# Pooling products in three rounded parts, and the new tokens' small transposes padded to 128 rows

## The chip, the cores and the metric

The kernel runs on one core of a Trainium2 chip. The metric is the device time of one execution in microseconds (us); the time given for a kernel is the median of its runs.

## What is computed

One inference step of a decoder with a single layer, for a prompt of 1024 positions and for 8 new tokens (one for each of 8 samples). The input is normalised and projected; the columns of the projection go to an attention group (three branches: compressed blocks, selected blocks, window) and to a pooling group; each is gated, both are projected back, added to the input and normalised. The change touches the pooling group, the attention of the new tokens, and the positional rows of the compressed branch. Cut from the reference:

```python
def pool_mixer(u_ext, n_out, w_pool, pool_scale):
    ...
    mean = (csum[:, le - n_out + 1:] - lo) / (end[:, None] - start).astype(f32)
    d = (mean - uf[:, le - n_out:]).reshape(n, n_out, N_POOL_GROUPS, POOL_GROUP_DIM)
    y = jnp.einsum('nlgc,gcd->nlgd', d, w_pool).reshape(n, n_out, D_POOL)
    return y * pool_scale

def block(bi):                                   # of nsa_attention
    ...
    p_c = jnp.where(ok_c, jax.nn.softmax(jnp.where(ok_c, s_c, -MASK_BIG), axis=-1), 0.0)
    o_c = jnp.einsum('nkgqc,nckd->nqkgd', p_c, v_c)
    ...
    o_s = jnp.einsum('nkgqs,nkqsd->nqkgd', p_s, vg)
    ...
    o_w = jnp.einsum('nkgqs,nskd->nqkgd', p_w, wrows[:, :, 1])
    return gg[..., 0:1] * o_c + gg[..., 1:2] * o_s + gg[..., 2:3] * o_w
```

For the pooling group there are four groups of 128 channels with windows of 2, 4, 8 and 16 positions and one 128 x 128 matrix each. A new token attends to 256 cached positions in each of the selected and the window branch and to itself.

## The kernel before

Data lie with features or tokens on the 128 partitions. Products of full precision are made from rounded parts: a float32 value is copied to a rounded type (the high part, on ScalarE) and the rest is subtracted (the low part, on VectorE or GpSimd; `split_w`, lines 138 to 140), and a product is the sum of high by high, low by high and high by low, three TensorE instructions. A few products stay in plain float32: the pooling products and some small ones of the new tokens. The trace shows a plain float32 product as two passes.

The stages in order of time: the input is normalised and transposed, and keys, values and gates are projected token by token (0 to 109 us); keys and values are compressed (to 194 us); the queries are projected (lines 490 to 505); then, from about 194 to 293 us, the four pooling groups, with the attention of the new tokens in between; then the attention over the prompt in 32 units (8 tiles of 128 queries by 4 pairs of heads), with the gate path (lines 918 to 948) and the output projection as filling work, to the end.

A pooling group (loop from line 761) loads a tile of projection weights, projects 1032 tokens (1024 and the 8 new ones) in three chunks of 384, 384 and 264 columns (`feat_unit`, lines 359 to 367), adds up windows on VectorE, takes the differences `dd` (line 792), projects its gate in three chunks, and multiplies `dd` with its matrix `pw`, chunk by chunk (line 809). The result is scaled, gated and stored.

The attention of the new tokens (`decode`, lines 509 to 662) runs at a raised priority ahead of the pooling in the program. It makes scores of the compressed branch (line 570), a softmax, and a transpose of it (575); then for each of the other two branches it transposes the new keys (586), gathers the cached rows of 8 samples, two at a time, in buffers `kvx` (599 to 605), transposes the keys (607), splits keys and values (612 to 618), makes the scores (621, 622), a softmax, transposes it (632) and its column for the new token (634), and multiplies with the values (645) and the new value (653). The sum is transposed at the end (656). The transposes at 575, 632, 634 and 656 have 64 rows (8 samples by 8 heads), the one at 586 has 8, and that of the positional rows (409) has 32.

The order on each engine is made by a planner that simulates a time line from costs of its own and takes what is ready by priority; instructions then run in that order on each engine, each waiting for its inputs. So a change of some costs can move the order of other work too. Loads from memory go through SP's queue in order, gathers through GpSimd's. A tile that reuses the memory of an earlier one waits for that one's last readers. The first attention unit's softmax tiles lie where the new tokens' tiles lay.

Of the kernel before, what the change touches and what calls it, by code (L numbers as in the profile page):

```python
# [22 lines left out]
# pacing of the filling products: steps per block of attention (gate path, output), blocks added per unit,  # L23
# steps at the start, lag in products
# [3 lines left out]
# the rows of the output weights, by half of their columns, that take the place of each chunk of x  # L28
# [13 lines left out]
def hybrid_step_kernel(ctx, tc, xp, xs, ccmp, cslc, cwin, spool, ptab, norm_g, w_in, cmp_pe, cmp_w1,  # L42
# [34 lines left out]
    # DRAM scratch  # L77
# [5 lines left out]
    # constants  # L83
# [8 lines left out]
    def ptr_rms(pool, ssq, n, name):  # L92
        """(ssq / D + eps) ** -0.5 for a [n, 1] column."""
# [5 lines left out]
    # persistent data  # L99
# [56 lines left out]
    pe32 = keep.tile([32, 128], F32, name="pe32")  # L156
# [7 lines left out]
    nc.sync.dma_start(pe32, cmp_pe)  # L164
    def spread_g(h):
        """The norm's weights from the first partition to all."""
        cs = slice(h * 512, h * 512 + 512)
        p = ps_any()
        nc.tensor.matmul(p, ones, gb[0:1, cs], start=True, stop=True)
        if h:  # L170
            nc.scalar.activation(gb[:, cs], p, AF.Copy)
        else:
            nc.vector.tensor_copy(gb[:, cs], p)

    # masks
# [12 lines left out]
    # normalised x, transposed, as high and low parts  # L188
# [37 lines left out]
    # token-major projections: compressed, selected and window keys and values, gate logits  # L226
# [114 lines left out]
    # a token before the end of the first compressed block has no compressed branch  # L341
# [28 lines left out]
    def silu2(out, src):  # L370
        """2 * silu(src)"""
# [3 lines left out]
    # page indices: row of 2 tokens each  # L375
# [12 lines left out]
    # compressed keys and values, prompt and samples  # L388
# [20 lines left out]
    nc.tensor.transpose(p[:, :32], pe32, ident[:32, :32])  # L409
# [79 lines left out]
    # queries  # L489
# [19 lines left out]
    def decode():  # L509
        """One new token per sample."""  # L510
        dp = des.enter_context(tc.tile_pool(name="dp", bufs=1, reuse_waits="tile"))
        # queries, one column per head and sample; qx: high parts, then low parts, per sample
# [7 lines left out]
        def diag(ap):  # L520
            """The columns of each sample's own heads in [b, 2, 64] columns: [p, b, h]."""
# [15 lines left out]
        for br in range(2):  # L537
            kn = dp.tile([NB, 256], F32, name=f"knew{br}")
            nc.sync.dma_start(kn, (nslc_s, nwin_s[:, 255])[br])
# [18 lines left out]
        Pd = [dp.tile([64, 258], F32, name=f"pd{br}") for br in range(2)]  # L558
        Pd = [Pd[0], Pd[1], Pd[0]]
# [15 lines left out]
        nc.tensor.transpose(p[:, :64], Pd[0][:, :128], ident[:64, :64])  # L575
        PcT = dp.tile([128, 64], F32, name="PcT")
        nc.vector.tensor_copy(PcT, p[:, :64])
        od = dp.tile([64, 128], F32, name="od")
# [3 lines left out]
        for br in range(2):  # L582
            vx = []
            kn = dp.tile([128, NB], F32, name="kn", bufs=2)
            p = ps_s("dkn")
            nc.tensor.transpose(p[:, :NB], knew[br][:, :128], ident[:NB, :NB])
            nc.vector.tensor_copy(kn, p[:, :NB])
            sp = ps_s("dS")
            for b in range(0, NB, 2):
# [8 lines left out]
                for bb in range(2):  # L598
                    f = dp.tile([128, 512], F32, name="kvx", bufs=4)
# [9 lines left out]
                    # high and low parts of the values  # L609
# [18 lines left out]
            dd = dp.tile([64, NB], F32, name="dd", bufs=2)  # L628
            nc.vector.tensor_scalar(dd, bmask, P_[:, 256:257], None, op0=OP.mult)
            p = ps_s("dptr")  # L630
            for par in range(2):
                nc.tensor.transpose(p[:, par * 64:(par + 1) * 64], P_[:, par * 128:(par + 1) * 128],
                                    ident[:64, :64])
            nc.tensor.transpose(p[:NB, 128:192], dd, ident[:64, :64])
            for par in range(2):
                src = p[:, par * 64:(par + 1) * 64].rearrange("p (b h) -> p b h", b=NB)
# [3 lines left out]
            E_ = dp.tile([NB, 64], F32, name="dE", bufs=2)  # L640
            nc.vector.tensor_copy(E_, p[:NB, 128:192])
# [11 lines left out]
            nc.tensor.matmul(p[:64, :128], E_, knew[br][:, 128:256], start=True, stop=True)  # L653
            nc.vector.tensor_add(od, od, p[:64, :128])
        p = ps_s("dOt")
        nc.tensor.transpose(p[:, :64], od, ident[:64, :64])
# [548 lines left out]
```

## Time and profile before

| | us |
|---|---|
| median of 3 runs | 656.16 |
| lowest, highest | 655.71, 656.98 |
| the profiled execution: span from the first to the last instruction | 654.4 |
| TensorE products busy | 627.6 (96%) |
| TensorE weight loads busy | 581.6 (89%) |
| VectorE busy | 426.0 (65%) |
| ScalarE busy | 361.0 (55%) |
| GpSimd busy | 266.8 (41%) |

The profile is of one execution; its own time is not given beside its span, so the median stands for it, 1.8 us above the span. Busy time counts the modelled length of an instruction, and products overlap in it. In the rows, PE is TensorE, DVE is VectorE, ACT is ScalarE, POOL is GpSimd, SP is the engine whose queue issues most loads; L809 is line 809; `out<-in` names the tiles written and read; of a product, `64*128` gives the rows and columns of its weights and `64x64` the rows and columns that are streamed.

### The profile page before, as it was taken

How to read it: one execution, taken by the hardware profiler on the slowest of the kernel's cores; microseconds unless marked ns; L12 is line 12 of the kernel's file. 1: busy time of each engine (PE TensorE's matmuls, PEld its weight loads, DVE VectorE, ACT ScalarE, POOL GpSimd, SP SyncE). 2: the span in 40 equal slices, each digit the busy share in tenths (PEclk: the TensorE clock that was granted, in tenths of full speed). 3: DMA queues.
4: the chain of work that ended last, by engine and by line, in shares of the span. 5: the costliest groups of instructions: out<-in, count | busy, mean ns of one | idle time of the engine just before them, and what ended most of it. 6: DMA issues, size and time to landing. Idle time of an engine off the chain costs nothing. (4 is left out here: it accounts for less than half of the span.)

```text
span 654.4 us, 12214 instructions
## 1 busy us (share of the span) xinstructions
PE 627.6 (96%) x4141; PEld 581.6 (89%) x4141; DVE 426.0 (65%) x1306; ACT 361.0 (55%) x930; POOL 266.8 (41%) x410
## 2 busy tenths in 40 slices
PE   6995999999999999999999899999999999999995
PEld 4995999999999999998999888788899999988984
DVE  5741234555526547575797998779888788877652
ACT  5652233444413234325788787767587677665641
POOL 5153001431207424104565666736454445454511
PEclk9997999999999999999999999999999999999999
DMA  8432302984524342243313437212022030101001
GB/s 274 147 100 56 102 16 76 310 274 118 162 72 135 84 142 70 94 132 98 97 33 98 130 113 238 86 34 82 32 83 97 18 97 18 65 17 66 18 34 64
DMA packets 65677, 65.14 MB, mean 100 GB/s; under 512 B 6423, under 2 KB 56927, under 8 KB 65575
## 3 DMA queue, kind: packets, MB, share of 16 engines
q1 hardware_dynamic: 55599, 44.53, 22.8%
q0 software_dynamic: 3968, 12.76, 6.0%
q10 hardware_dynamic: 6048, 7.08, 3.0%
q8 instruction: 33, 0.54, 0.3%
q14 instruction: 29, 0.24, 0.1%
HBM read 50.99 MB, written 15.68 MB: 102 GB/s over the span
## 5 line engine op out<-in xcount | busy, mean ns | idle before, releaser
L756 POOL TENSOR_SCALAR Ps<-Ps,sm,gates 128x64 f32<-128x64 f32 (+1 forms) x120 | 75.3, 639 | 111.1 <-DVE sm L752 77.3
L736 PE MATMUL S<-KT,qt 128*128 128x320 f32 (+10 forms) x400 | 98.3, 347 | 1.9 <-DVE sm L699 1.8
L859 DVE TENSOR_TENSOR pl<-tp,ph 128x512 fp32r<-128x512 f32 (+1 forms) x136 | 89.9, 670 | 13.5 <-ACT ph L858 12.4
L858 ACT ACTIVATE ph<-tp 128x512 fp32r<-128x512 f32 (+1 forms) x136 | 76.6, 579 | 35.2 <-PE tp L853 28.2
L365 PE MATMUL pa<-x,ws_hi 128*128 128x384 f32 (+1 forms) x288 | 93.6, 325 | 0.0
L366 PE MATMUL pa<-x,ws_hi 128*128 128x384 f32 (+1 forms) x288 | 92.8, 322 | 0.0
L367 PE MATMUL pa<-x,ws_lo 128*128 128x384 f32 (+1 forms) x288 | 92.6, 322 | 0.0
L750 ACT ACTIVATE Ps<-Ps,sm 128x64 f32<-128x64 f32 (+8 forms) x128 | 70.6, 554 | 28.2 <-DVE sm L748 26.7
L995 PE MATMUL pj<-wo,mh 128*128 128x512 f32 x256 | 82.6, 400 | 0.0
L871 PE MATMUL O<-pl,V 128*128 128x256 f32 x264 | 77.7, 311 | 1.0 <-DVE pl L859 0.9
L870 PE MATMUL O<-ph,V 128*128 128x256 f32 x264 | 74.2, 295 | 0.0
L736 PEld LDWEIGHTS S<-KT,qt 128*128 128x128 f32 x400 | 63.9, 189 | 8.8 <-DVE sm L699 2.8
L244 PE MATMUL pa<-w_hi,x 128*128 128x256 f32 (+1 forms) x192 | 57.7, 301 | 0.2 <-DVE V L317 0.2
L246 PE MATMUL pa<-w_hi,x 128*128 128x256 f32 (+1 forms) x192 | 56.9, 296 | 0.4 <-DVE x L217 0.4
L245 PE MATMUL pa<-w_lo,x 128*128 128x256 f32 (+1 forms) x192 | 56.1, 293 | 0.0
L366 PEld LDWEIGHTS pa<-x,ws_hi 128*128 128x128 f32 x288 | 54.2, 188 | 0.4 <-issue 0.2
L365 PEld LDWEIGHTS pa<-x,ws_hi 128*128 128x128 f32 x288 | 54.2, 188 | 0.3 <-DVE us L776 0.2
L367 PEld LDWEIGHTS pa<-x,ws_lo 128*128 128x128 f32 x288 | 54.1, 188 | 0.3
L871 PEld LDWEIGHTS O<-pl,V 128*128 128x128 f32 x264 | 49.7, 188 | 4.8 <-DVE pl L859 3.0
L870 PEld LDWEIGHTS O<-ph,V 128*128 128x128 f32 x264 | 49.9, 189 | 2.0 <-ACT ph L858 0.2
L995 PEld LDWEIGHTS pj<-wo,mh 128*128 128x128 f32 x256 | 45.1, 188 | 7.0 <-PE S L736 0.4
L995 PE MATMUL pj<-wo,ml 128*128 128x512 f32 x128 | 50.6, 395 | 0.1
(279 smaller groups left out, 1530.9 us busy)
## 6 DMA issues: line engine op xcount, KB each, us to landing
ws_raw<-in_w_in SPq DMA_DIRECT2D x32, 256.0 KB
qt<-q_d SPq DMA_DIRECT2D x64, 128.0 KB
x_t<-in_x_prompt SPq DMA_DIRECT2D x8, 512.0 KB
wo_raw<-in_w_out SPq DMA_DIRECT2D x8, 512.0 KB
r<-in_x_prompt SPq DMA_DIRECT2D x8, 512.0 KB
out<-r SPq DMA_DIRECT2D x7, 512.0 KB
q_d<-qhl ACTq DMA_DIRECT2D x8, 384.0 KB
out<-kvf ACTq DMA_DIRECT2D x5, 512.0 KB
```

The source lines that it names most:

```text
L244: nc.tensor.matmul(p[:n, :cn], xh[c][:, k, ts_], hi[:, k, :cn], start=k == 0, stop=False)
L365: nc.tensor.matmul(p[:, :n], hi[:, k, :], xh[c][:, k, :], start=k == 0, stop=False)
L366: nc.tensor.matmul(p[:, :n], hi[:, k, :], xl[c][:, k, :], start=False, stop=False)
L367: nc.tensor.matmul(p[:, :n], lo[:, k, :], xh[c][:, k, :], start=False, stop=k == 7)
L736: nc.tensor.matmul(S[:, :ln], qt[:, f, h, :], KT[:, kv, k0 + a:k0 + a + ln], start=f == 0, stop=f == 1)
L750: nc.scalar.activation(regs[br], regs[br], AF.Exp, bias=sm[:, hh, 1, br:br + 1], accum_out=sm[:, hh, 2, br:br + 1])
L756: nc.gpsimd.tensor_scalar(regs[br], regs[br], sm[:, hh, 3, br:br + 1], gsrc[:, k:k + 1], op0=OP.mult, op1=OP.mult)
L858: nc.scalar.activation(ph[:, :m], tp[:, :m], AF.Copy)
L859: nc.vector.tensor_sub(pl[:, :m], tp[:, :m], r32(ph[:, :m]))
L870: nc.tensor.matmul(O[:, :256], vv, ph[:, a * 256:(a + 1) * 256], start=False, stop=False)
L871: nc.tensor.matmul(O[:, :256], vv, pl[:, a * 256:(a + 1) * 256], start=False, stop=last)
L995: nc.tensor.matmul(p, a[:, k % 4, :], w, start=first and kk == 0, stop=last and kk == 2)
```

## The change

The pooling products become sums of three products of rounded parts: the matrix of a group is loaded in the group (one load of a 128 x 128 matrix in place of one for all four) and split on ScalarE and GpSimd; each chunk of the differences is split on ScalarE and VectorE into one buffer, `dx`. The tiles that the small transposes and the new value's product read get 128 rows, of which the unused ones are set to zero by GpSimd once; the transposes then take all 128 rows and use the full identity matrix (the product at 653 keeps its 64 weight columns, the transpose at 634 its 8). For the space, the gather buffers `kvx` go from four to three, and `kn` from two to one. Comments are dropped.

```diff
-    pe32 = keep.tile([32, 128], F32, name="pe32")
+    pe32 = keep.tile([128, 128], F32, name="pe32")
+    nc.gpsimd.memset(pe32, 0.0)
...
-    nc.sync.dma_start(pe32, cmp_pe)
+    nc.sync.dma_start(pe32[:32], cmp_pe)
...
-    nc.tensor.transpose(p[:, :32], pe32, ident[:32, :32])
+    nc.tensor.transpose(p[:, :128], pe32, ident)
...
-            kn = dp.tile([NB, 256], F32, name=f"knew{br}")
-            nc.sync.dma_start(kn, (nslc_s, nwin_s[:, 255])[br])
+            kn = dp.tile([128, 256], F32, name=f"knew{br}")
+            nc.gpsimd.memset(kn, 0.0)
+            nc.sync.dma_start(kn[:NB], (nslc_s, nwin_s[:, 255])[br])
...
-        Pd = [dp.tile([64, 258], F32, name=f"pd{br}") for br in range(2)]
-        Pd = [Pd[0], Pd[1], Pd[0]]
+        Px = [dp.tile([128, 258], F32, name=f"pd{br}") for br in range(2)]
+        for P_ in Px:
+            nc.gpsimd.memset(P_, 0.0)
+        Px = [Px[0], Px[1], Px[0]]
+        Pd = [P_[:64] for P_ in Px]
+        ddx = dp.tile([128, NB], F32, name="ddx")
+        nc.gpsimd.memset(ddx, 0.0)
+        Ex = dp.tile([128, 64], F32, name="Ex")
+        nc.gpsimd.memset(Ex, 0.0)
...
-        nc.tensor.transpose(p[:, :64], Pd[0][:, :128], ident[:64, :64])
+        nc.tensor.transpose(p[:, :128], Px[0][:, :128], ident)
...
-        od = dp.tile([64, 128], F32, name="od")
+        odx = dp.tile([128, 128], F32, name="od")
+        nc.gpsimd.memset(odx, 0.0)
+        od = odx[:64]
...
-            kn = dp.tile([128, NB], F32, name="kn", bufs=2)
+            kn = dp.tile([128, NB], F32, name="kn", bufs=1)
             p = ps_s("dkn")
-            nc.tensor.transpose(p[:, :NB], knew[br][:, :128], ident[:NB, :NB])
+            nc.tensor.transpose(p[:, :128], knew[br][:, :128], ident)
...
-                    f = dp.tile([128, 512], F32, name="kvx", bufs=4)
+                    f = dp.tile([128, 512], F32, name="kvx", bufs=3)
...
-                nc.tensor.transpose(p[:, par * 64:(par + 1) * 64], P_[:, par * 128:(par + 1) * 128],
-                                    ident[:64, :64])
-            nc.tensor.transpose(p[:NB, 128:192], dd, ident[:64, :64])
+                nc.tensor.transpose(p[:, par * 128:(par + 1) * 128], Px[br + 1][:, par * 128:(par + 1) * 128],
+                                    ident)
+            nc.tensor.transpose(p[:NB, 256:384], ddx, ident)
...
-            nc.tensor.matmul(p[:64, :128], E_, knew[br][:, 128:256], start=True, stop=True)
+            nc.tensor.matmul(p[:64, :128], Ex, knew[br][:, 128:256], start=True, stop=True)
...
-        nc.tensor.transpose(p[:, :64], od, ident[:64, :64])
+        nc.tensor.transpose(p[:, :128], odx, ident)
...
-    pw = pp.tile([128, 4, 128], F32, name="pw")
-    nc.sync.dma_start(pw, pool_w.rearrange("g c d -> c g d"))
...
+        pw = pp.tile([128, 128], F32, name="pw")
+        nc.sync.dma_start(pw, pool_w[g])
+        pwx = pp.tile([128, 2, 128], F32R, name="pwx")
+        split_w(pwx[:, 0], pwx[:, 1], pw, nc.gpsimd)
...
+            dx = pp.tile([128, 2, 384], F32R, name="dx")
+            split_w(dx[:, 0, :n], dx[:, 1, :n], dd[:, t0:t0 + n])
             p = ps_t("yp")
-            nc.tensor.matmul(p[:, :n], pw[:, g, :], dd[:, t0:t0 + n], start=True, stop=True)
+            for k, (a, b) in enumerate(((0, 0), (1, 0), (0, 1))):
+                nc.tensor.matmul(p[:, :n], pwx[:, a], dx[:, b, :n], start=k == 0, stop=k == 2)
```

## Rows read from the trace of the kernel before

**Rows 1.** Busy time by stretch: us, each engine's busy us (instructions), granted clock, DMA.
```profile
100.00:300.00 200.00, 199.57 (x1284) 191.93 (x1282) 108.94 (x289) 71.40 (x163) 57.65 (x78) 1.00 0.46 139
300.00:450.00 150.00, 145.29 (x975) 131.70 (x975) 122.23 (x492) 116.92 (x355) 90.43 (x151) 1.00 0.33 99
```

**Rows 2.** Time line, TensorE, first group's pooling products: start us, us, engine, line.
```profile
205.90 1.90 PE L809 MATMUL yp<-ws,pw 128*128 128x384 f32 x6
...
207.81 0.34 PE L367 MATMUL pa<-x,ws_lo 128*128 128x384 f32 x1
207.98 0.33 PE L365 MATMUL pa<-x,ws_hi 128*128 128x384 f32 x1
```

**Rows 3.** Time line, TensorE, around the compressed branch's transpose.
```profile
213.50 0.28 PE L367 MATMUL pa<-x,ws_lo 128*128 128x264 f32 x1
213.62 0.28 PE L365 MATMUL pa<-x,ws_hi 128*128 128x264 f32 x1
213.83 0.27 PE L575 MATMUL dpt<-ident,pd 64*128 64x64 f32 x1
...
214.26 0.28 PE L367 MATMUL pa<-x,ws_lo 128*128 128x264 f32 x1
```

**Rows 4.** Time line, TensorE, from the new value's product to transposes of 128 rows.
```profile
250.42 0.43 PE L653 MATMUL dOn<-knew,dE 8*64 8x128 f32 x2
250.78 0.22 PE L586 MATMUL dkn<-ident,knew 8*128 8x8 f32 x1
250.94 0.28 PE L770 MATMUL ut<-ident,u 128*15 128x128 f32 x1
251.06 0.27 PE L771 MATMUL ut<-ident,u 128*8 128x128 f32 x1
```

**Rows 5.** Time line, TensorE, products ahead of and behind the first branch's transposes.
```profile
243.47 0.28 PE L366 MATMUL pa<-x,ws_hi 128*128 128x264 f32 x1
...
244.23 0.28 PE L365 MATMUL pa<-x,ws_hi 128*128 128x264 f32 x1
```

**Rows 6.** Time line, TensorE, the same around the second branch's transposes.
```profile
277.33 0.34 PE L365 MATMUL pa<-x,ws_hi 128*128 128x384 f32 x1
...
278.67 0.34 PE L365 MATMUL pa<-x,ws_hi 128*128 128x384 f32 x1
```

**Rows 7.** Time line, TensorE, the last transpose among the last group's pooling products.
```profile
290.64 0.81 PE L809 MATMUL yp<-ws,pw 128*128 128x384 f32 x2
291.38 0.27 PE L656 MATMUL dOt<-ident,od 64*128 64x64 f32 x1
291.58 0.91 PE L809 MATMUL yp<-ws,pw 128*128 128x384 f32 x2
```

**Rows 8.** Time line, TensorE, around the positional rows' transpose.
```profile
100.29 0.29 PE L246 MATMUL pa<-w_hi,x 128*128 128x280 f32 x1
...
101.03 0.29 PE L245 MATMUL pa<-w_lo,x 128*128 128x280 f32 x1
```

**Rows 9.** Time line, TensorE, the new tokens' compressed scores and their successor.
```profile
201.61 0.43 PE L570 MATMUL dsc<-Kcs,qs 128*64 128x128 f32 x2
201.97 0.45 PE L365 MATMUL pa<-x,ws_hi 128*128 128x384 f32 x1
```

**Rows 10.** Grouped by line and shape, 150 to 300 us: busy us, mean ns | idle before.
```profile
L497 ACT ACTIVATE qhl<-pa 128x384 fp32r<-128x384 f32 x2 | 1.0, 492 | 2.7 <-PE pa L367 2.7
L498 DVE SCALAR_TENSOR_TENSOR qhl<-pa,qhl 128x384 fp32r<-128x384 f32 x2 | 1.1, 558 | 1.3 <-ACT qhl L497 1.0 <-issue 0.3
```

**Rows 11.** Time line, GpSimd: a fill, the fifth gather, the next value split.
```profile
197.97 1.84 POOL L518 MEMSET px<- 128x2048 f32 x1
...
218.74 1.01 POOL L601 DMA_INDIRECT kvx<-in_cache_slc_kv,idx  x1 [7.95 <-PE dkt L607]
...
222.68 0.74 POOL L613 TENSOR_TENSOR vx<-kvx,vx 128x256 fp32r<-128x256 f32 x1 [1.69 <-ACT vx L612]
```

**Rows 12.** Time line, TensorE: the last value products, the prompt's first scores.
```profile
284.52 1.93 PE L645 MATMUL dO<-vx,px 128*128 128x256 f32 x15
...
296.94 0.81 PE L736 MATMUL S<-KT,qt 128*128 128x192 f32 x6
```

More of the change, by code (lines that the diff above doesn't have):

```diff
@@ L627, in decode @@
             P_ = Pd[br + 1]
-            dd = dp.tile([64, NB], F32, name="dd", bufs=2)
-            nc.vector.tensor_scalar(dd, bmask, P_[:, 256:257], None, op0=OP.mult)
+            nc.vector.tensor_scalar(ddx[:64], bmask, P_[:, 256:257], None, op0=OP.mult)
             p = ps_s("dptr")
             for par in range(2):
-                nc.tensor.transpose(p[:, par * 64:(par + 1) * 64], P_[:, par * 128:(par + 1) * 128],
-                                    ident[:64, :64])
-            nc.tensor.transpose(p[:NB, 128:192], dd, ident[:64, :64])
+                nc.tensor.transpose(p[:, par * 128:(par + 1) * 128], Px[br + 1][:, par * 128:(par + 1) * 128],
+                                    ident)
+            nc.tensor.transpose(p[:NB, 256:384], ddx, ident)
             for par in range(2):
-                src = p[:, par * 64:(par + 1) * 64].rearrange("p (b h) -> p b h", b=NB)
+                src = p[:, par * 128:par * 128 + 64].rearrange("p (b h) -> p b h", b=NB)
                 ph, pl = (diag(px[:, par, 0, part, :]) for part in range(2))
@@ L639, in decode @@
                 nc.vector.tensor_sub(pl, src, r32(ph))
-            E_ = dp.tile([NB, 64], F32, name="dE", bufs=2)
-            nc.vector.tensor_copy(E_, p[:NB, 128:192])
+            nc.vector.tensor_copy(Ex[:NB], p[:NB, 256:320])
             p = ps_s("dO")
```

## The prediction

> **What bounds the kernel now.** I read the busy times by stretch first. Each row gives a stretch's busy time per engine. From 100 to 300 us, which holds all the work that the change touches but one fill and one load, TensorE is busy 199.57 of 200 us at a granted clock of 1.00 (the 2.4 GHz level), VectorE 108.94, ScalarE 71.40 and GpSimd 57.65 [rows 1]. From 300 to 450 us TensorE still has 145.29 of 150. So TensorE sets the end, and an edit is worth what it does to the distance between starts on TensorE; work added to the other three is free while TensorE has something else next in its order. A "busy" time will not do for the price: the products overlap (each 384-column product is shown as 0.33 us but the next starts 0.17 us later), so below I take starts from the time line and subtract neighbours at their usual distance. That distance is 0.17 us for a product of 384 moving columns [rows 2] and 0.12 us for one of 264 [rows 3], both in the three-part form that the change gives to the pooling products.
>
> **Pooling products.** Each of the four groups has three plain float32 products, shown as two passes each. In the first group the six passes start at 205.90 and the second product behind them at 207.81, which is 0.17 us after the one in between: 207.81 - 205.90 - 0.17 = 1.74 us [rows 2]. In three rounded parts it is 6 x 0.17 + 3 x 0.12 = 1.38 us (1.40 with 0.174 from the longer run of such products). Gain 0.34 to 0.36 per group; I take 0.33, as three parts come each with a weight load of its own, so 1.3 us for four. Bounds: 0.9 (if the three parts of a chunk cost 10% over the feature products) and 1.45.
>
> **Padded transposes.** A lone transpose of 64 rows is dear by its neighbours. The compressed branch's (L575): the product ahead starts at 213.62, the second one behind at 214.26; 0.64 less two products of 0.12 is 0.40 us [rows 3]. It starts 0.21 us after its predecessor where 0.12 is usual, and the stream behind it is pulled apart too. A transpose that uses all 128 rows starts 0.11 to 0.12 us after its predecessor and pushes nothing: L770 at 250.94, L771 at 251.06 [rows 4]. So padded, the 0.40 becomes 0.11: 0.29 gained. In the same way:
> the first branch's three (L632 twice, L634): 243.47 to 244.23 is 0.76, less 0.24 for two products, 0.52; against 3 x 0.11 = 0.33: 0.19 [rows 5].
> The second branch's three, where a product came between them: 277.33 to 278.67 is 1.34, less 3 x 0.17, 0.83; against 0.33: 0.50 [rows 6].
> The last one (L656), between passes of the pooling products: the third pass starts 0.94 after the first where two passes of about 0.32 make 0.64, and the pair behind is shown 0.91 long where the pair ahead is 0.81: 0.40; against 0.11: 0.29 [rows 7].
> The positional rows (L409): 100.29 to 101.03 is 0.74, less 0.13 + 0.13 for two products of 280 columns and 0.11 for the full transpose ahead: 0.37; against 0.11: 0.26 [rows 8].
> Sum 0.29 + 0.19 + 0.50 + 0.29 + 0.26 = 1.5 us. The upper bound is 1.7; the lower is in the rivals.
>
> **Edits that I cost at nothing on TensorE.** The new keys' transpose (L586, 8 rows) stands behind the new values' product (L653) and takes 0.16 us to its successor [rows 4]; padded it takes 0.11 and itself pays for coming after a product that stays apart: 0 to 0.1 us for both. That product keeps 64 weight columns: its two passes take 250.42 to 250.78, 0.36 us, with 8 rows [rows 4], and the scores (L570), the same with 128 rows by 64 columns, 201.61 to 201.97, 0.36 us [rows 9]. So 128 rows instead of 8 buy nothing there; bounds 0 and, should it run like a full one (2 x 0.11), 0.3 for both branches. I take 0.
>
> **Work added beside.** Twelve splits of the pooled differences: a ScalarE copy and a VectorE subtraction as those of the queries, 0.49 and 0.56 us for 384 columns [rows 10], 12.6 us in all over some 90 us, on engines with over 40% free there. They hide under the next group's input products, which are hundreds and need neither; without that cover each of the eight waits for the only split buffer costs 0.49 + 0.56 = 1.05 us (the first chunk's split lies behind nothing but the differences). Four splits of the pooling weights, on ScalarE and GpSimd, each a third of that, are wanted once a group. The pooling weights' one load becomes four on SP's queue, between loads of projection weights; each holds up a projection load by its issue alone, and TensorE waited for no load in that stage [rows 1]: nothing. Seven GpSimd fills of at most 258 columns at the start of the new tokens' part, some 1,230 columns: the fill of 2048 columns takes 1.84 us [rows 11], so 1.1 us, perhaps 1.7 with seven starts. Behind them on GpSimd are the gathers and the masks that the first scores wait for; SP's two loads of the new keys now wait for a fill, and behind these on SP stand a gate load and then the projection loads. This puts the new tokens' chain back by up to 1.7 us, under TensorE's products, while TensorE's own order saves it as much. The fill of the positional rows at the start (128 columns) and its load behind it: at most 0.2 us.
>
> **Three gather buffers for four.** This is the step I trust least. The fifth gather waited for a transpose to free its buffer (7.95 us of GpSimd idle ending at 218.74) and its values were split at 222.68, 3.9 us later [rows 11]. With three, the fourth gather of a branch waits as well: one more round of up to 3.9 us in each of two branches, or nothing where TensorE's order has the next pair's transposes later anyway. Behind this wait on GpSimd stand the value splits of the tiles already there, and for them wait the value products. I take 1 us a branch, which is the chain's and not TensorE's: 0 in the sum, and rival (c) if it is more.
>
> **Sum.** 1.3 + 1.5 = 2.8 us. The profiled execution's span is 654.4 us, the median 656.16, so 1.8 us lie around the span. Span 654.4 - 2.8 = 651.6; time 656.16 - 2.8 = 653.4 us. A measurement of this kernel tells about 0.2% (1.3 us) from no change, so this would be seen, by a factor of two.
>
> **Rivals.**
> (a) Padding gives nothing: the distances around the small transposes come from waits and not from the shape. Then the padded ones only stream more columns: eight of 64 become 128 and three of 8 or 32 become 128, at most 8 x 0.05 + 3 x 0.11 = 0.7 us more. 656.16 - 1.3 + 0.7 = 655.6 us. Against it: three lone transposes in three places cost 0.40, 0.40 and 0.37 us [rows 3, 7, 8], which waits would hardly repeat, and the full-shape one costs 0.11 [rows 4]. The Trainium skill, TensorE: Matmul & The Clock Gate, "Why this matters for your kernels", says that a single product of 32 rows takes the same time as one of 128; by that rule this rival would hold. The Trainium skill, TensorEngine Tiling, "Key Properties", says that a change of tiling mode drains the engine; the rows agree with the second.
> (b) Part of the gain goes back: the split buffer of the last group has only the gate path behind it, and two of its waits show: 2 x 1.05 = 2.1 us, 656.16 - 2.8 + 2.1 = 655.5; or the order, which is laid out anew around the changed times, loses 1 to 3 us in the attention, where 150 - 145.29 = 4.7 us are already idle [rows 1]: 654.4 to 656.4.
> (c) Slower: the attention starts too late. Its tiles go where the new tokens' tiles lay, and the last of these are given up by the last value products, at 284.52 + 1.93 = 286.45; the first scores start at 296.94, 10.5 us behind [rows 12]. Say they keep that distance. If the third buffer costs both rounds, 7.8 us, less some 1.5 us that TensorE has gained by then, the scores start at 303.2, while the pooling ends at 290.64 + 2.0 - 2.8 = 289.8 (its six passes and the transpose took 2.0 us [rows 2, 7]). Between lie 13.4 us. Ahead of the scores the order has one piece of the gate path, 24 products of 0.17, 4.2 us; with a second 8.4. The hole is then 5.0 us: 656.16 - 2.8 + 5.0 = 658.4 us, and with one piece 662.6. It decides from where the scores start over 8.4 us behind the last pooling product. For it: the chain's last transpose already stands between the last pooling products [rows 7]. Against it: 10.5 us is more than a load needs, so the first microseconds of delay may be free.
>
> **How the numbers follow.** The full sum, 652.3 to 654.8: 0.50. (a) 0.08. (b) 0.24, of which 0.05 is still faster by over 0.2%. (c) 0.18. Faster 0.50 + 0.05 = 0.55; within 0.2%: 0.08 + 0.17, 0.25; slower: 0.18 and 0.02 of (b), 0.20. The forecast is the likeliest, 653.4. The range: at the lower end the upper bounds (1.45 + 1.7 + 0.4 = 3.6 us, 652.6) and a lucky order, 652.0; at the upper a hole of 4.4 us, a little under (c): 657.8. What lies outside is most of (c) and a little of the first case, 2 in 10.
>
> **What would show it.** Right: three-part pooling products at 0.17 and 0.12 us, a slot of 1.4 us a group; the padded transposes 0.11 us behind their predecessors, with no pulled-apart products after them; the stretch from 100 us to the first score product 2.8 us shorter with TensorE as full as before. Wrong: TensorE idle before a pooling product with the split named as releaser (b); first scores later than 297 us and TensorE idle ahead of them (c); 0.2 us around a 128-row transpose (a).

## The result and the profile after

The changed kernel takes 672.22 us (672.01 to 672.82) against 655.94 us in the same set of runs: ratio 1.0242, 95% interval 1.0229 to 1.0256. It is 16.3 us slower where 2.8 us faster was forecast, and lies above the range. Its span is 671.1 us, where before had 654.4.

Busy time by stretch, columns as in [rows 1]; the first two lines answer them:

```profile
100.00:300.00 200.00, 196.95 (x1286) 192.29 (x1285) 112.79 (x279) 76.41 (x172) 61.05 (x89) 0.99 0.46 140
300.00:450.00 150.00, 137.34 (x875) 123.75 (x876) 113.08 (x465) 106.03 (x330) 79.75 (x139) 0.95 0.31 97
...
296.00:302.00 6.00, 1.71 (x7) 1.36 (x7) 1.33 (x8) 0.76 (x2) 1.32 (x2) 0.56 0.77 239
302.00:308.00 6.00, 5.81 (x22) 5.84 (x23) 1.22 (x13) 1.21 (x6) 1.27 (x3) 0.59 0.00 1
308.00:313.00 5.00, 3.82 (x26) 3.26 (x26) 3.19 (x26) 3.74 (x19) 1.51 (x4) 1.00 0.20 57
313.00:318.00 5.00, 5.00 (x30) 4.89 (x29) 0.73 (x3) 0.89 (x3) 2.20 (x6) 0.66 0.18 51
420.00:430.00 10.00, 6.97 (x33) 6.15 (x33) 7.87 (x30) 9.07 (x25) 6.06 (x7) 0.83 0.29 101
```

Two of these stretches in the kernel before:

```profile
302.00:308.00 6.00, 5.83 (x41) 5.46 (x40) 2.88 (x20) 2.78 (x12) 4.18 (x11) 1.00 0.57 153
420.00:430.00 10.00, 10.00 (x67) 8.07 (x67) 8.47 (x29) 6.49 (x17) 1.80 (x4) 1.00 0.07 21
```

TensorE does 875 instructions between 300 and 450 us in place of 975. Two holes show: at 296 to 318 us, where attention begins, and at 420 to 430 us, where the gate path ends. In both the granted clock falls: at the first 0.56 and 0.59 are close to the 1.2 GHz level (0.66 at 313 to 318 us, with 1.00 in between), so that a "busy" 5.81 us holds 22 products where before did 41.

The prices on which the sum stood are met. Time line of TensorE, answers to [rows 8, 3, 5, 2, 4]:

```profile
100.73 0.27 PE L325 MATMUL kp<-ident,kvf 128*128 128x128 f32 x1
100.84 0.27 PE L410 MATMUL pe_ps<-ident,pe 128*128 128x128 f32 x1
100.87 0.38 PE L245 MATMUL pa<-w_hi,x 128*128 128x280 f32 x1
101.08 0.29 PE L246 MATMUL pa<-w_lo,x 128*128 128x280 f32 x1
...
214.02 0.29 PE L367 MATMUL pa<-x,ws_hi 128*128 128x264 f32 x1
214.15 0.27 PE L584 MATMUL dpt<-ident,pd 128*128 128x128 f32 x1
214.18 0.37 PE L368 MATMUL pa<-x,ws_lo 128*128 128x264 f32 x1
214.38 0.29 PE L366 MATMUL pa<-x,ws_hi 128*128 128x264 f32 x1
...
245.41 0.34 PE L366 MATMUL pa<-x,ws_hi 128*128 128x384 f32 x1
245.58 0.38 PE L642 MATMUL dptr<-ident,pd 128*128 128x128 f32 x2
245.98 0.27 PE L644 MATMUL dptr<-ident,ddx 128*8 128x128 f32 x1
246.26 0.33 PE L366 MATMUL pa<-x,ws_hi 128*128 128x384 f32 x1
...
206.34 0.34 PE L368 MATMUL pa<-x,ws_lo 128*128 128x384 f32 x1
206.51 0.34 PE L823 MATMUL yp<-dx,pwx 128*128 128x384 f32 x1
206.69 0.34 PE L366 MATMUL pa<-x,ws_hi 128*128 128x384 f32 x1
...
254.00 0.43 PE L662 MATMUL dOn<-knew,Ex 128*64 128x128 f32 x2
254.36 0.33 PE L597 MATMUL dkn<-ident,knew 128*128 128x128 f32 x1
```

Worked as in the prediction: the positional rows' transpose costs 0.11 us (was 0.37), the compressed branch's 214.38 - 214.02 - 2 x 0.12 = 0.12 (0.40), the first branch's three 246.26 - 245.41 - 3 x 0.17 = 0.34 (0.52; 0.33 forecast), a rounded pooling product 0.17 to 0.18. The new value's product still takes 0.36 us with 128 rows, as forecast. None of this is where the time went.

Where it went is seen on VectorE. Its time line where attention starts, first the kernel before, then the changed one. L699 and L706 are the first unit's score reductions, L910 and L924 the first write of the gate path into its buffer `za`; brackets give the idle time ahead and what ended it:

```profile
294.38 0.61 DVE L812 SCALAR_TENSOR_TENSOR bb<-yp,psc,sz 128x384 f32<-128x384 f32 x1
297.57 0.23 DVE L699 CUSTOM_DVE_ANT_0 Ps<-S,mc 128x64 f32<-128x64 f32 x1 [2.57 <-PE S L736]
...
299.42 0.29 DVE L699 CUSTOM_DVE_ANT_0 Pw<-S,mslc 128x128 f32<-128x128 f32 x1
299.63 0.68 DVE L910 SCALAR_TENSOR_TENSOR za<-zt,pj 128x128 f32<-128x128 f32 x3
```

```profile
296.41 0.73 DVE L670 COPY as_t<-dOt 64x16 f32<-64x16 f32 x4 [0.48 <-PE dOt L665]
301.36 0.68 DVE L924 SCALAR_TENSOR_TENSOR za<-zt,pj 128x128 f32<-128x128 f32 x3 [4.22 <-DMA b_d<-bb]
301.96 0.21 DVE L706 CUSTOM_DVE_ANT_0 Ps<-S,mc 128x64 f32<-128x64 f32 x1
```

The store that this write waits for is issued by GpSimd, first in the kernel before, then in the changed one:

```profile
295.67 0.59 POOL L818 DMA_DIRECT2D b_d<-bb  x1 [0.30 <-POOL bb L817]
```

```profile
297.50 0.58 POOL L832 DMA_DIRECT2D b_d<-bb  x1 [0.30 <-POOL bb L831]
```

`za` lies on the memory from which the last pooling group is stored (`bb`), so its first write waits for that store. Before, nine reductions stood ahead of it and the store had landed by then, at 298.68 us; the gate write waited for nothing. In the changed kernel the store lands at 301.23 us, 2.5 us later. And VectorE's order has the gate write ahead of all reductions: 4.22 us pass, and behind it stand the reductions, for these the exponentials, the probability transposes and the scores' banks. TensorE waits with them:

```profile
302.19 0.66 PE L939 MATMUL pj<-x,ws_hi 128*128 128x384 f32 x1 [3.76 <-DVE za L924]
302.64 0.53 PE L940 MATMUL pj<-x,ws_hi 128*128 128x384 f32 x1
302.96 0.53 PE L941 MATMUL pj<-x,ws_lo 128*128 128x384 f32 x1
```

and comes back at the slow clock, products 0.32 us apart in place of 0.17.

### The profile page after: what moved, and what is told of

Same layout as the page of the kernel before. It is cut to its first block, busy times and chain, and to the rows that moved or that the text cites. A ratio compares the mean times of both kernels' runs of the same rounds, so it can differ in the third digit from the quotient of the medians.

```text
span 671.1 us, 12294 instructions
## 1 busy us (share of the span) xinstructions
PE 633.7 (94%) x4153; PEld 589.0 (88%) x4153; DVE 434.5 (65%) x1318; ACT 368.4 (55%) x946; POOL 268.8 (40%) x422
## 5 line engine op out<-in xcount | busy, mean ns | idle before, releaser
L743 PE MATMUL S<-KT,qt 128*128 128x320 f32 (+10 forms) x400 | 100.5, 350 | 8.1 <-DVE sm L706 7.0
L873 DVE TENSOR_TENSOR pl<-tp,ph 128x512 fp32r<-128x512 f32 (+1 forms) x136 | 89.7, 669 | 11.6 <-ACT ph L872 10.9
L140 DVE TENSOR_TENSOR ws_lo<-ws_raw,ws_hi 128x512 fp32r<-128x512 f32 x40 | 27.0, 704 | 36.5 <-ACT ws_hi L139 32.5
```

Of the source, the lines that this page charges most:

```text
L743: nc.tensor.matmul(S[:, :ln], qt[:, f, h, :], KT[:, kv, k0 + a:k0 + a + ln], start=f == 0, stop=f == 1)
L873: nc.vector.tensor_sub(pl[:, :m], tp[:, :m], r32(ph[:, :m]))
```

## Experiments

Each run is a whole kernel with the edit shown or named. The ratio is to the kernel before, run again in the same set (medians of 656 to 657 us). To place a loss in time I value the TensorE instructions that are left at a given moment with the distance that each has to its successor in the kernel before; the difference is how far a kernel lags behind it, whatever order it chose. The first 110 us differ from execution to execution by -1.5 to +1.7 us for the same instructions, so the moments are counted from one early product (113.69 us before) in each. Lag in us at that moment of the kernel before:

| kernel | 300 | 320 | 400 | 430 | 500 | median, us | ratio (95%) |
|---|---|---|---|---|---|---|---|
| changed | 1.7 | 8.0 | 10.2 | 14.6 | 15.6 | 672.22 | 1.0242 (1.0229-1.0256) |
| e1 gate buffer moved | -0.8 | 1.6 | 4.7 | 5.2 | 6.1 | 665.66 | 1.0140 (1.0120-1.0159) |
| e2 padding alone | -0.1 | 1.6 | 4.8 | 7.2 | 7.4 | 665.15 | 1.0137 (1.0110-1.0163) |
| e3 buffers alone | 2.5 | 6.3 | 6.4 | 9.2 | 9.4 | 668.39 | 1.0183 (1.0161-1.0205) |
| e4 pooling alone | 2.4 | 10.3 | 15.1 | 18.6 | 18.6 | 677.35 | 1.0306 (1.0257-1.0354) |
| e5 one edge | 0.6 | 4.8 | 3.8 | 7.3 | 7.6 | 663.74 | 1.0108 (1.0083-1.0132) |
| e6 moved, one edge | 0.7 | 2.5 | 0.3 | 4.2 | 4.9 | 661.95 | 1.0078 (1.0057-1.0100) |
| e7 padding, one edge | 0.6 | 2.0 | 0.9 | 2.4 | 2.2 | 658.59 | 1.0028 (1.0013-1.0042) |
| e8 before, buffer moved | 0.0 | -0.1 | 0.1 | 0.2 | 0.2 | 656.99 | 0.9998 (0.9987-1.0009) |
| e9 two edges | 0.6 | 3.2 | 2.6 | 4.8 | 4.9 | 660.71 | 1.0056 (1.0036-1.0075) |
| e10 three edges | -0.7 | 2.4 | 0.3 | 2.3 | 2.1 | 658.87 | 1.0037 (1.0023-1.0051) |
| e11 padding, two edges | 0.2 | 1.7 | 0.1 | 2.1 | 2.0 | 658.03 | 1.0018 (1.0004-1.0032) |
| e15 three edges, moved | -0.7 | 2.5 | 0.5 | 2.7 | 2.6 | 659.72 | 1.0042 (1.0029-1.0054) |
| e16 three edges, copies later | -0.7 | 2.4 | 0.3 | 1.0 | 1.1 | 657.38 | 1.0021 (1.0001-1.0041) |
| e18 padding, three edges | 0.0 | 0.7 | 0.3 | 0.5 | 0.4 | 656.21 | 1.0003 (0.9990-1.0015) |

The lags are estimates, good to about 1 us and to 2 or 3 us where the loss is large: counted from the same early product, the spans themselves end 16.7 us later than before for the changed kernel, 10.5 for e3, 20.4 for e4, 2.4 for e10 and 0.3 for e18. So the changed kernel loses 6 to 8 us up to 320 us, some 3 more up to 360 (lag 10.9 there; e5 doesn't have these), and some 4 between 400 and 430.

**e1: the wait for the store.** The gate's buffer is placed elsewhere, so that its first write doesn't wait for the store.

```diff
-    zap = ctx.enter_context(tc.tile_pool(name="zap", bufs=1, reuse_waits="tile"))
-    za = zap.tile([128, 4, TOK], F32, name="za")
     at2 = ctx.enter_context(tc.tile_pool(name="at2", bufs=2, reuse_waits="tile"))
+    zap = ctx.enter_context(tc.tile_pool(name="zap", bufs=1, reuse_waits="tile"))
+    za = zap.tile([128, 4, TOK], F32, name="za")
```

> The changed kernel, with the gate's tile za placed elsewhere, behind the value tiles of the attention, so that it no longer takes the memory from which the last pooling group is stored. Theory S (store): the hole at 298 to 302 us is VectorE's first gate write waiting for that store to land, in front of the first reductions in VectorE's order. Then TensorE's wait of 3.8 us goes, the clock stays at 1.00 there, the first unit ends 7 to 11 us earlier (313 instead of 322.4 us) and the time is 661 to 665 us. Rival L (late chain): the three gather buffers bring the new tokens' chain in late, the store is a bystander; then the time stays at 670 to 673 us. Rival P (pooling): the single split buffer of the pooling products is late; it too stays at 670 to 673 us.

665.66 us, just above theory S's range: 6.6 us come back, the lag at 320 us falls from 8.0 to 1.6, and the granted clock is 1.00 from 296 to 308 us. The wait is confirmed as the main loss at the start of attention. 6 us and more stay.

**e2 to e4: which part brings the order.** The change's parts alone: padding with the four gather buffers; the fewer buffers (`kvx` and `kn` together) and nothing else; pooling with the buffers that it needs for its space (three gather buffers, `kn`, `dd` and `dE` single).

```diff
e3, on the kernel before:
-                    f = dp.tile([128, 512], F32, name="kvx", bufs=4)
+                    f = dp.tile([128, 512], F32, name="kvx", bufs=3)
 ...
-            kn = dp.tile([128, NB], F32, name="kn", bufs=2)
+            kn = dp.tile([128, NB], F32, name="kn", bufs=1)
```

> The kernel before with the padding alone (plain float32 pooling products, four gather buffers, two kn). By the sum of the prediction 1.5 us less: 654.5 us. Theory S: VectorE's order here too has the first gate write, with its wait for the store, ahead of the first reductions; so a hole of some microseconds and 658 to 668 us. Rivals L and P: neither the buffers nor the split are in it, so 654 to 655 us.

> The kernel before with three gather buffers for four and one kn for two, nothing else. Theory S: the order again has the gate write first, so 658 to 670 us, with the wait for the store in the trace. Rival L: the whole loss is here, 668 to 675 us, and the chain's last value products end about 7 us later than before (293 instead of 286 us). Rival P: 656 us, no change.

> The kernel before with the pooling products in three parts alone; for the space three gather buffers and one buffer each of kn, dd and dE; no padding. Theory S: gate write first in the order, 665 to 674 us. Rival L: like the run with the buffers alone. Rival P: the whole loss, 670 to 675 us, while the run with the buffers alone shows none. On TensorE each group's products should take 1.4 us where they took 1.74.

665.15, 668.39 and 677.35 us: each loses, padding too, which on TensorE only shortens work (beside it are GpSimd's fills and one buffer each of `ddx` and `Ex`). In e3 and e4 VectorE's gate write waits for the store (2.0 and 4.6 us), and in all three it stands ahead of the first reductions in VectorE's order; in the kernel before it stands behind nine. The times don't decide between the theories: e3's lies in the ranges of S and of L, and e4's above all of them. In e2 the gate write, at 296.19 us, waits for no store, the clock stays at 1.00, and most of the loss comes behind 320 us; TensorE does 48 gate-path products ahead of the first scores there, in place of 24. So theory S holds for the order in all three, for the wait only in e3 and e4. No single part is the culprit; with any of them the order is another one, and the order of before was a good one.

**e5 to e8: order or wait.** An ordering edge that waits for nothing puts the first gate write behind the first unit's six reductions; alone (e5), with the buffer moved (e6), on padding alone (e7). e8 moves the buffer in the kernel before.

```diff
e5:
 ...
             nc.vector.scalar_tensor_tensor(z if both else a, z, 1.0, p[:, c:c + m], op0=OP.add, op1=OP.mult)
+            if not half_done:
+                after(nc.cur_bb.bb.instructions[-1], reds[5])
```

> The changed kernel with one ordering edge more, which waits for nothing: VectorE's first gate write (za) stands behind the six score reductions of the first unit, as in the kernel before. The place of za and its wait for the last group's store stay. Theory O (the loss at the handover is the order alone: the wait is covered once the reductions stand ahead of it): first unit's end at 311 to 314 us in place of 322.4, time 659 to 663 us, the clock between 298 and 322 us at the 2.4 GHz level. Theory W (the wait itself costs, wherever it stands, since the gate path that gives TensorE its fill work hangs on it): 668 to 672 us. In neither case does the stretch at 400 to 440 us get better.

> The changed kernel with both: the gate's buffer placed elsewhere (no wait for the store), and the same ordering edge. Theory O: nothing beyond the better of the two alone, 659 to 664 us, since each takes the same stall away. Rival: order and wait each cost by themselves, and their gains add: 655 to 658 us. If the rest lies at 400 to 440 us, the first unit ends at 311 to 313 us and the time is still 660 us or more.

> Padding alone (665.2 us without the edge) with the same ordering edge. Theory O: the first unit ends at 311 us or earlier, time 656 to 659 us; if the prediction's 1.5 us for the padding come through as well, 654 to 655 us. Theory W: 663 to 666 us.

> The kernel before with the gate's buffer placed elsewhere, so that its first write doesn't wait for the store; its order on VectorE stays (reductions first). Theory O: the wait was hidden in the kernel before, so 655 to 658 us, no difference. Rival: the move by itself changes the time (other tiles wait in its place, the order is laid out anew): over 660 us, and then the gain of the same move in the changed kernel can't be read as the price of the wait.

The edge alone gives back 8.5 us (663.74), somewhat less than theory O said, and padding alone comes to 658.59, in O's range. e6, with both, comes to 661.95: the gains don't add, as theory O said, and its 1.8 us over e5 are no clear difference. e8 shows none: in the kernel before there was no wait to take away, so moving the buffer costs or gains nothing by itself, and e1 can be read as the price of the wait. In e5 the wait is still there, 1.8 us long, but with the first six reductions past. So the loss at this place was the order's, in the changed kernel through this wait, in padding alone without it. What is left in e5 begins at the same place: the first unit's output is copied from 311.95 us on (311.31 before, 322.42 in the changed kernel), but the gate path is late, and against theory O the clock is low again (0.52 and 0.63 at 296 to 308 us).

**e9 to e11: the late decode chain.** A reason lay further ahead, in the new tokens' last branch. VectorE's time line in the changed kernel: the softmax steps (L636 to L576, L639) with the last pooling group's window sums (L791) between them:

```profile
277.46 0.41 DVE L636 TENSOR_TENSOR pd<-dS,pd 64x257 f32<-64x257 f32 x1
277.79 1.21 DVE L791 TENSOR_TENSOR ws<-ws 128x1024 f32<-128x1024 f32 x1
278.93 0.40 DVE L572 TENSOR_REDUCE dst<-pd 64x1 f32<-64x257 f32 x1
...
281.79 0.14 DVE L573 TENSOR_SCALAR dst<-dst 64x1 f32<-64x1 f32 x1
281.87 1.20 DVE L791 TENSOR_TENSOR ws<-ws 128x1024 f32<-128x1024 f32 x1
...
285.31 0.21 DVE L639 TENSOR_SCALAR ddx<-bmask,pd 64x8 f32<-64x8 f32 x1
```

That is 8.1 us from the first to the last step. Before, they took 3.2 us (271.74 to 274.93) and the sums came behind; first and last step, and under them the first step in e3:

```profile
271.74 0.42 DVE L625 TENSOR_TENSOR pd<-dS,pd 64x257 f32<-64x257 f32 x1 [4.08 <-ACT pd L624]
...
274.71 0.22 DVE L629 TENSOR_SCALAR dd<-bmask,pd 64x8 f32<-64x8 f32 x1
```

```profile
275.62 0.42 DVE L625 TENSOR_TENSOR pd<-dS,pd 64x257 f32<-64x257 f32 x1 [3.67 <-ACT pd L624]
```

So the softmax starts late as well, by 5.7 us in the changed kernel, by 3.9 with the fewer buffers alone and by 2.0 with padding alone (273.72). In e3 that isn't the sums' doing, which come behind its softmax, and the edges take only some of it back (275.57 in e10). The last value products end at 293.70 us in place of 286.45 [rows 12], and TensorE has used its gate-path products as filler ahead of them, which before lay behind and covered what comes between the last transpose and the first scores. Edge two keeps the window sums behind that softmax; edge three keeps TensorE's gate-path products behind the last transpose; e11 is padding alone with the first two.

```diff
 edge two:
 ...
             nc.vector.tensor_add(nx[:, H0:H0 + T], cur[:, H0:H0 + T], cur[:, H0 - step:H0 + T - step])
+            if g == 3:
+                after(nc.cur_bb.bb.instructions[-1], ddx_at[-1])
 edge three:
 ...
                     nc.tensor.matmul(p[:, :n], hi[:, k, :], xh[c][:, k, :], start=k == 0, stop=False)
+                    if k == 0 and not half_done:
+                        after(nc.cur_bb.bb.instructions[-1], dot_at[0])
```

> The changed kernel with the edge of the run before (gate write behind the first unit's reductions; 663.7 us) and a second one: the last pooling group's window sums on VectorE (four of 1.2 us) stand behind the last decode group's softmax, as in the kernel before, and no longer between its steps. Theory L (what remains is that the decode chain ends late, at 296 us in place of 293, with the gate-path fill used up before it, so that nothing covers the handover): its two probability transposes come at 278 to 281 us in place of 285.5 and the last value product ends by 290 us; but the gate-path products still stand ahead of the value products, so only part is given back: 659 to 663 us. Rival B (three gather buffers keep the chain late whatever VectorE's order is): no change, 663 to 665 us.

> The run with two edges and a third: TensorE's first gate-path product stands behind the last decode transpose (dOt), as in the kernel before, so that 24 dense products lie between the decode's end and the first score product. Theory L: the handover has cover again, the clock stays at the 2.4 GHz level at 296 to 308 us, the first unit ends at 310 to 312 us and the time is 654 to 658 us. Rival: the products now missing further ahead leave TensorE idle there for the 2 to 4 us that the probabilities take, and nothing is gained on the run with two edges: 660 to 664 us. If the handover is cured and the time is still 658 us or more, the rest lies at 400 to 440 us.

> Padding alone with the first two edges (658.6 us with the first alone). Theory L: here the gate-path products fall behind the value products by themselves, the handover is covered, and what the prediction gave the padding comes through: 653.5 to 656 us. Rival: the padding's 1.5 us are no gain even then, since what follows the handover is bound by something else: 656.5 to 659 us.

660.71, 658.87 and 658.03 us. With the second edge the softmax takes 2.6 us (276.10 to 278.66), with the third the gate-path products stand behind the last transpose again. e10's time line, from the value products (L655) to the first scores (L756), with the 24 gate-path products (L957 to L961) between:

```profile
285.82 2.05 PE L655 MATMUL dO<-vx,px 128*128 128x256 f32 x16
287.80 0.43 PE L663 MATMUL dOn<-knew,Ex 128*64 128x128 f32 x2
288.16 0.99 PE L838 MATMUL yp<-dx,pwx 128*128 128x384 f32 x3
289.77 0.62 PE L838 MATMUL yp<-dx,pwx 128*128 128x384 f32 x2 [0.61 <-ACT dx L139]
290.24 0.30 PE L666 MATMUL dOt<-ident,od 128*128 128x128 f32 x1
290.30 0.42 PE L957 MATMUL pj<-x,ws_hi 128*128 128x384 f32 x1
...
294.58 0.34 PE L961 MATMUL pj<-x,ws_lo 128*128 128x384 f32 x1
294.75 0.81 PE L756 MATMUL S<-KT,qt 128*128 128x192 f32 x6
```

The clock holds to 302 us now (1.00 in 296 to 302) but not behind it (0.72 in 302 to 308). Theory L holds for the chain and in part for the cover; e9 is in its range, e10's forecast of 654 to 658 us is missed by 0.9 us, and e11's by 2, inside its rival's: at 400 us both kernels have caught up with the kernel before (0.3 and 0.1), and lose 2 us behind that.

**e12 to e14: the pace of the gate path.** e10 with 24 gate-path steps owed at the start of attention in place of 12; e10 with 0.9 steps per block in place of 0.8; the latter on the kernel before.

```diff
-NZ, NO, C0, OW, PLAG = 0.8, 0.5, 2, 12, 100
+NZ, NO, C0, OW, PLAG = 0.9, 0.5, 2, 12, 100
```

> The run with three edges (658.9 us: 2 to 5 us ahead of the kernel before up to the 12th unit, behind it after the 15th), with 24 gate-path steps owed at the start of attention in place of 12. Theory G (the lead is given back where the gate path ends, since the gate path itself is not ahead: its last tanh at 400.6 us against 400.2 before, and the output weights can only be split behind it): the last gate tanh moves 2 to 3 us ahead, the first output product from 414 to 411 us or earlier, time 655 to 658 us. Rival H (the lead is given back because attention's units alone have too little work to fill TensorE with, wherever the gate path stands): no change or slower, 658.5 to 661 us.

> The run with three edges, with the gate path's pace raised from 0.8 to 0.9 steps per block. Theory G: last gate tanh at 390 to 397 us, first output product by 409 us, time 654 to 657 us. Rival H: fill is used up sooner, TensorE waits for the output weights and for reductions from 395 us on, the granted clock falls there, 659 to 662 us.

> The kernel before with the same raised pace, as the other half of the comparison: what the pace does by itself. If it gains here as much as in the run with three edges, the gain there is the pace's and no cure of what the change broke. Theory G: 655 to 658 us, no gain, since the gate path and the attention are in step here. Rival: 652 to 654.5 us.

660.51 us (1.0047, 1.0027 to 1.0067), 659.73 (1.0039, 1.0024 to 1.0054) and 665.01 (1.0120, 1.0100 to 1.0139). Theory G is not borne out, nor put to its test: counted from the common early product, the last gate tanh came no sooner (401.1 and 401.5 us in e12 and e13, 400.9 in e10). The first output product did, by 2.0 and 1.6 us, and the time got no better. The times lie in rival H's ranges, but not for its reason: e12 and e13 lose less at 400 to 430 us and more behind 500 us. The control, outside both its forecasts, says the most: one constant of the pace, without any change of the work, costs the kernel before 8 us.

**e15 to e17: what is left.** e15 is e10 with the gate's buffer moved as in e1; e16 is e10 with the bulk copies of the cached state issued behind the 21st unit in place of the 15th, e17 the same on the kernel before; e18 is padding alone with all three edges.

```diff
e16, e17:
-        if x == 14:
+        if x == 20:
```

> The run with three edges and the gate's buffer placed elsewhere. If the wait for the last group's store still costs something with the order cured (the first gate write stands behind it, and three gate products' banks with it): 655 to 657.5 us. If the order was all: 658 to 660 us, no difference.

> The run with three edges (658.9 us), with the bulk copies of the window and pool state issued behind the 21st unit in place of the 15th, so that they don't share the DMA engines with the last output weights. Theory D (what is lost at 400 to 420 us hangs on the landing of the last output weights, 6.9 us from issue in place of 6.2 us in the kernel before, and on what is queued behind them): weights land in under 4 us, the first output product comes 2 to 3 us sooner, time 655 to 657.5 us. Rival A (it hangs on the engines' order there, ScalarE's and VectorE's, which the changed kernel lays out otherwise): 658 to 660 us.

> The kernel before with the same move of the copies, as the control: if it gains as much, the gain is that of the copies alone and says nothing of what the change broke. Theory D: the last weights land sooner here too, 654 to 656 us. Rival A: no difference, or slower by a new order, 656 to 660 us.

> Padding alone (four gather buffers) with all three edges; it had 658.0 us with two, with the last decode transpose still behind the gate-path products. Theory L: with the decode's end ahead of them the clock stays at the 2.4 GHz level at 296 to 308 us and 1 to 2 us come back, 655.5 to 657 us. If the padding's gain of 1.5 us were to show in the end: 654 to 655.5 us. Rival: the order after 380 us decides, 657.5 to 659 us.

659.72 us: no difference from e10, so with the order cured the store's wait shows no price. 657.38 us for e16, and the control at 656.35 (0.9996, 0.9985 to 1.0007) gains nothing. The last output weights are split once they have landed; ScalarE's time line in e10 and, below, in e16, tanh of the last gate piece and the splits:

```profile
400.56 0.39 ACT L931 ACTIVATE zt<-pj 128x264 f32<-128x264 f32 x1 [0.16 <-PE pj L961]
408.23 1.15 ACT L981 ACTIVATE wo<-wo_raw 128x512 fp32r<-128x512 f32 x2 [2.19 <-DMA wo_raw<-in_w_out]
```
```profile
400.69 0.39 ACT L931 ACTIVATE zt<-pj 128x264 f32<-128x264 f32 x1 [0.17 <-PE pj L961]
406.06 1.14 ACT L981 ACTIVATE wo<-wo_raw 128x512 fp32r<-128x512 f32 x2
```

The splits come 2.2 us sooner, as theory D has it, and the first output product follows the tanh by 11.4 us in place of 13.7 (11.1 before). The lag at 430 us goes from 2.3 to 1.0; but the two medians' intervals overlap, so the landing of these weights is a likely part of the last 2 us and not proven. e18 lands at 656.21 us, the time of the kernel before, without the copies moved: with four buffers and the order kept, its first output product follows the tanh by 10.8 us. No version beats the kernel before by what these runs can tell.

## Why the prediction was wrong

**What bounds the kernel.** Right: TensorE is full up to the handover in both kernels (in the changed one it is idle for 1.5 us between 100 and 298 us). But from this it was concluded that an edit is worth what it does to the distances on TensorE, and that work on the other engines is free while TensorE has something else next. That is the step that failed: it holds only while the order on the engines stays. The runs showed in its place one VectorE instruction that stood ahead of the reductions and waited 4.22 us for a store (6.6 us of time by e1), and 13.4 of the 16.3 us came back by ordering edges alone.

**The sum of 2.8 us.** Each price that can be read off the new trace was right within 0.03 us. As an earlier start of attention it shows in part: e10's first scores come at 294.75 us, with three pooling products of 0.36 us in all still to come, so 1.83 us ahead of [rows 12]; its early product was 0.36 us ahead, and 0.61 us of idle lies in it (the split `dx`, as rival (b) had it). So 1.83 - 0.36 + 0.61 = 2.1 us of work saved, of the 2.5 forecast behind that product (2.8 less 0.26 for the positional rows). For e18 it is 1.84 - 1.45 + 0.63 (idle ahead of the last transpose) = 1.0, of 1.24. At 300 us 0.7 us and nothing are left of it, and at 500 us nothing of either: the saving doesn't reach the end.

**Edits that I cost at nothing.** The new value's product: right (0.36 us). The one buffer `dx`: 0.51 us of TensorE idle in the changed kernel, half of one wait of the two feared. The three gather buffers, "the step I trust least", were put at 0 in the sum: with the single `kn` they cost 12 us alone (e3; the two were not taken apart). The feared round of 3.9 us is there, in the start of the last softmax, and padding alone starts it 2.0 us late, where 1.7 was put on the fills. But as a delay they are not the loss: e10 keeps that lateness and loses 2.3 us. The last value products of the changed kernel end 7 us later, and padding alone, with four buffers, has them 6 us later too.

**The rivals.** (a) falls. The Trainium skill's sentence in TensorE: Matmul & The Clock Gate, "Why this matters for your kernels", that a single product of 32 rows takes the same time as one of 128 is not at odds with the trace as to the product itself: the one of 64 rows is shown as 0.27 us [rows 3], padded as 0.27 too. But it doesn't give what a single one costs in a stream of 128-row products: 0.37 us with 32 rows, 0.11 us with 128, at the same place.

(b) had the right cause, an order laid out anew, and a price of 1 to 3 us drawn from TensorE's 4.7 us of idle in attention. This term is the one that was mis-sized most: the edges alone give back 13.4 us. The order did not lose a little everywhere: it put one instruction that waits for a store ahead of the first reductions, pulled a softmax apart and used up TensorE's filler ahead of the handover.

(c) had the right place, "the attention starts too late", and named a hole between the pooling and the scores. In the changed kernel there is no such hole: the first scores start at 296.23 us, 0.7 us ahead of before. The hole comes six score products later, from VectorE's order. In e3, with the fewer buffers alone, the first scores do start late, at 303.98 us, and 3.56 us of TensorE idle lie ahead of them; but its releaser is the same gate write, not the new tokens' tiles. What I had left out: a look at who waits on VectorE at the handover. The trace of before has the gate write at 299.63 us and the landing of the store at 298.68: a wait hidden by one microsecond, which would have been a rival with a place and a price.

**The second loss.** Not foreseen. Behind 400 us the gate path has no more products to fill with and the output weights aren't there; the changed kernel waits 2.9 us for one reduction there at a granted clock of 0.83. That stretch is tender in the kernel before too: in e14, where only the pace differs, TensorE waits 3.4 us at once between 390 and 430 us. What exactly sets it in e10 stays open between the weights' landing and the engines' order.

## What to carry to other kernels

Where a planner lays out the engines' order from costs, a change of some costs or buffers can change the order everywhere: before adding up the savings, look in the trace for the instructions that are placed just late enough to find their input ready (a buffer's reuse behind a store above all), and name who queues behind them. When such a kernel gets slower, tie back the few orders that the trace shows as moved, one at a time; here three edges that wait for nothing gave back 13.4 of 16.3 us. A saving on the bounding engine has to outlast the next stages to be worth something: here 1 to 2 us saved ahead of attention were gone by its end.

## What the runs showed of the hardware

After 3.76 us of idle TensorE's products came 0.32 us apart, at the 1.2 GHz level, where 0.17 is usual; in e7 idle gaps of 0.74, 0.53 and 0.22 us among the first scores lie ahead of products 0.32 us apart, while in the kernel before, where gaps of 0.41 and 0.22 us come behind 24 dense products, the granted clock stays at 1.00. A store of 516 KB took 3.0 us from its issue to landing before (295.67 to 298.68) and 3.7 us in the changed kernel (297.50 to 301.23). A plain float32 product with 64 weight columns costs 0.36 us for two passes whether its streamed matrix has 8 or 128 rows, and of a transpose with 128 rows and 8 weight columns (L644) the successor starts 0.03 us behind it, as behind the full one (L584).
